# A two-layer decoder with retrieved experts: modulation chunks on GpSimd and ScalarE, 15 weight chunks ahead, and 160 dense tokens in both layers

## The chip, the cores and the metric

The kernel runs on one core of a Trainium2 chip. The metric is the device time of one execution in microseconds. Engines are named as in the profile: PE (matrix multiplications), DVE (VectorE), ACT (ScalarE), POOL (GpSimd) and SP (SyncE, which here only issues transfers). Each engine works through its own instructions in their order and waits for others by semaphores. Transfers between the chip's memory and the core's SBUF are issued by SP, ACT and POOL, and carried by 16 DMA engines.

## The reference

A residual stream of 256 tokens x 1024 channels goes through two layers, in float32. Each layer mixes the tokens, then sends each token through experts that it picks itself (128 x 128 = 16384 experts of one neuron, 8 heads x 16 picks for each token):

```python
def hybrid_layer(x, c_act, ...):
    mod = (c_act @ w_ada + b_ada)[:, None, :]
    sh1, sc1, g1, sh2, sc2, g2 = jnp.split(mod, 6, axis=-1)
    h = rms_norm(x, norm1_g) * (1 + sc1) + sh1
    proj = h @ w_in
    ...
    x = x + g1 * (merged @ w_out)
    h2 = rms_norm(x, norm2_g) * (1 + sc2) + sh2
    x = x + g2 * peer_ffn(h2, peer_wq, peer_sub_keys, peer_down, peer_up)
    return x

def block(t):                      # in peer_ffn
    q = (t @ w_pq).reshape(T, PEER_HEADS, 2, PEER_HALF)
    s = jnp.einsum('thpk,hpnk->thpn', q, sub_keys)
    top_s, top_i = lax.top_k(s, PEER_TOPK)
    cand_s = top_s[:, :, 0, :, None] + top_s[:, :, 1, None, :]
    cand_i = top_i[:, :, 0, :, None] * N_KEYS + top_i[:, :, 1, None, :]
    best_s, best_pos = lax.top_k(cand_s.reshape(...), PEER_TOPK)
    experts = jnp.take_along_axis(cand_i.reshape(...), best_pos, axis=-1)
    gate = jax.nn.softmax(best_s, axis=-1)
    act = jax.nn.gelu(jnp.einsum('td,thkd->thk', t, expert_down[experts]), approximate=False)
    return jnp.einsum('thk,thkd->td', gate * act, expert_up[experts])
```

## The kernel before

**Stages.** Each layer runs through mixing (16 weight chunks of w_in, the attention, convolution and gating work of a plan written out by hand, 8 chunks of w_out), retrieval (16 chunks of w_pq, the scores, the top 16 of each head), and the experts in two loops of 128 weight chunks: down (`chunk_mm`, matmuls in L345) and up (`add` in `combine`, L1137). A chunk is 128 x 1024 float32, 512 KB. Where one stage hands x to the next, ACT and DVE apply the modulation and the norm; below this is called the bridge.

**Dense and gathered tokens.** For T = `DENSE[layer]` tokens the experts' loops multiply with all 16384 experts and weigh the result by the gates (zero where an expert wasn't picked). For the other TS = 256 - T tokens the picked rows alone are gathered: a token has 128 picks, so POOL's indirect transfer (`fetch`, L1038) brings 128 rows, 512 KB, for one token. Rows of down are dotted with the token on DVE (`dot`, L1048), rows of up are weighed and added up on DVE (`add_row`, L1063). Gathered tokens are split into sets of powers of two (88 = 64 + 16 + 8, 96 = 64 + 32); `dot_spread` (L1020) and `spread_picks` (L1025) copy a set's tokens and picks over the partitions by 128/n small POOL transfers each. At chunk 125 of the up loop `folds` (L1143) adds each set's sum into the accumulators, so all rows must be added by then; the last two chunks' matmuls stand behind the folds.

**Buffers for rows.** `free` holds buffers, `fetch` starts a gather for each free one in order of tokens. `begin` is the down chunk at which the picks of the second token block are known; `where` for the first set and the first gathers come 4 chunks later. `start` is the chunk from which the gates of the dense tokens are worked off (`compare`, `factors`, `gate_mm`, `gate_use`). Before it, `dot` is called at the rate `DOT_SLOW` per chunk, after it at `DOT_RATE`.

**Weights.** `Src.seq` is the order of all chunks. They go through a ring of 7 buffers (`RAW`); SP issues the loads, and every second chunk of the experts is issued by ACT. "early" chunks don't use the ring: ten chunks of down (4 to 13 of the loop) are loaded into slots of SBUF (`AHEAD_AT`) while retrieval runs; seven of these slots (`PASSING`) serve as row buffers afterwards. Chunks that are split into a high and a low part (w_in, w_out, w_pq) are cast by ACT (`hi`, L265 and L267) and subtracted by DVE (`lo`, L258 and L260).

**Modulation.** The product c @ w_ada is 48 chunks for each layer, six groups of 8 (SH1, SC1, G1, SH2, SC2, G2). A chunk is multiplied and summed by one DVE instruction (`ada_chunk`, L218). Layer 0's chunks are loaded in its mixing; layer 1's are "asides": 40 in layer 0's experts (21 in the down loop, 19 in the up loop) and 8 in layer 1's, whose loads SP issues between the others.

**Retrieval's picks.** `fills` holds DVE's work for the two token blocks, block 1 first: `cand`, `top_cand`, `ranks`, `match`, `times`, `total` and `gate`; `run_fill` hands out some of it with each down chunk. `gate` (L902 on) subtracts the maximum, lets ACT take the exponential (L905), and sums it on DVE (L906). `expand` (L851) is a POOL cast.

Of the kernel before, what the change touches and what calls it, by code (L numbers as in the profile page):

```python
# [42 lines left out]
DENSE = (168, 160)  # L43
# [34 lines left out]
def hybrid_trunk(ctx: ExitStack, tc: tile.TileContext, x_in, c_in, vec_in, w_ada, w_in, w_out, w_pq,  # L78
# [81 lines left out]
    SLOTS_OPEN = [region(at * S, D) for at in (96, 100, 104)]  # L160
# [22 lines left out]
    class Src:  # L183
# [6 lines left out]
        asides = deque()  # L190
        ring = []
# [24 lines left out]

    def ada_chunk(layer, col, raw):
# [3 lines left out]
        if layer == 0 and col < G1:  # L221
            n = 1
        if (col + 1) % n == 0:
# [7 lines left out]
    def load_more(k):  # L231
        while Src.loaded < len(Src.seq) and (Src.ring[Src.loaded + 1] == Src.ring[Src.loaded]
                                             or Src.ring[Src.loaded] <= Src.ring[k + 1] + RAW - 2):
            dma_ahead(Src.loaded + 1)
# [73 lines left out]
    for layer in range(DEPTH):  # L308
# [3 lines left out]
        if layer == 0:  # L312
# [8 lines left out]
            body += mix(tail[:6], ada(0, [5])) + tail[6:]  # L321
        else:
            body += tail
# [8 lines left out]
        un = mix(un, aside[len(ASIDES_AT[layer]):], 4, 100)  # L332
# [200 lines left out]
    def mixing(layer, qg, update=None, late=None):  # L533
# [260 lines left out]
        other_form(layer)  # L794
        for n in range(2, 16):
            if n >= first:
# [7 lines left out]
        for n, k in enumerate(OUT_ORDER[layer]):  # L804
            if n == 4:
                nc.gpsimd.dma_start(R_KEYS, keys[layer])
            if n < 7:
# [15 lines left out]
    def retrieval(layer, update, late):  # L823
# [29 lines left out]
        narrowed = R_TE[:, 0, 0].rearrange("p j i k -> p (j i k)")[:, :256].rearrange("p (h j i) -> p h j i", h=8, j=2)  # L853
# [47 lines left out]
        def gate():  # L901
# [3 lines left out]
            nc.scalar.activation(sel[:, 2, :], sel[:, 2, :], AF.Exp)  # L905
            nc.vector.tensor_reduce(red[:, :8], g, op=OP.add, axis=AX.X)  # L906
# [46 lines left out]
        for d in range(DC):  # L953
            nc.scalar.activation(R_HX[:, d, :], R_H[:, d, :], AF.Identity, bias=shifts[:, d:d + 1])
        for pair in range(1, 8):
            if pair > 1:
# [7 lines left out]
        def rest():  # L964
            scores(7)
            for b in (1, 0):
# [4 lines left out]
                else:  # L971
                    fill.append((0.3, narrow))
                fill.append((0.95, lambda b=b: cand(b)))
                for h in (0, 4):
                    fill.append((3.8, lambda h=h: top_cand(range(h, h + 4))))
# [414 lines left out]
```

## Time and profile before

| what | us |
|---|---|
| median of 3 runs | 1615.31 (1614.17 to 1615.68) |
| profiled execution | 1619.4 |
| its span | 1617.7 |
| mixing and retrieval of layer 0 | 0 to 188.6 |
| down loop of layer 0 | 188.6 to 523.0 |
| up loop of layer 0 | 523.0 to 849.4 |
| mixing and retrieval of layer 1 | 849.4 to 1002.8 |
| down loop of layer 1 | 1002.8 to 1313.5 |
| up loop of layer 1 | 1313.5 to 1613.6 |

The stages are bounded by the first matmuls of each loop. Such a profile is read from the whole to the part: the busy shares and the transfer rate over the span say which resources are near their limit where; windows laid on the stages say what each carries; the waits of PE say which of them lets it stand still; and the timeline around the end of a stage says what came last.

### The profile page before, as it was taken

Reading aid. Unit: us, or ns where it says so; the run is one execution under the profiler, and the core shown is the slowest. Engines: PE = TensorE matmul, PEld = TensorE weight load, DVE = VectorE, ACT = ScalarE, POOL = GpSimd, SP = SyncE. Lnnn points to the kernel's source line nnn. Section 1 sums busy time; section 2 is a strip of 40 time slices with the busy share of each in tenths; the row PEclk is TensorE's granted clock in tenths of the full one; section 3 lists DMA queues with packets and bytes.
Section 4 is the critical chain, followed back from the end, with each engine's and each line's share of the span. In section 5 each row is a group of like instructions: output and inputs, shape, how many; then the busy total and the mean of one; then the engine's idle time right before and its main releaser. Section 6 shows DMA issues by size and latency. Waiting matters only on the chain.

```text
span 1617.7 us, 29030 instructions
## 1 busy us (share of the span) xinstructions
PE 1550.2 (96%) x11240; PEld 1514.8 (94%) x11240; DVE 1002.7 (62%) x2263; ACT 475.4 (29%) x1356; POOL 518.5 (32%) x467
## 2 busy tenths in 40 slices
PE   7999996999999999998979999989999999999996
PEld 6879996999999999998979899989999999999995
DVE  6778884777777444444436668859777754444435
ACT  2346311466654000000015763115655510000000
POOL 1000125533333544444400001145433444444441
PEclk9999998999999999999979999989999999999997
DMA  9998647999999999999955666499999999999995
GB/s 387 344 361 310 184 151 254 360 419 418 419 418 418 418 419 419 418 419 418 420 216 169 195 231 198 149 387 374 419 418 418 418 419 419 419 419 418 418 419 201
DMA packets 157082, 570.27 MB, mean 353 GB/s; under 512 B 18736, under 2 KB 19312, under 8 KB 155792
## 3 DMA queue, kind: packets, MB, share of 16 engines
q1 hardware_dynamic: 65232, 237.92, 38.4%
q0 software_dynamic: 56144, 201.41, 31.3%
q10 hardware_dynamic: 35568, 129.08, 20.2%
q8 instruction: 88, 1.44, 0.3%
q14 instruction: 50, 0.41, 0.1%
HBM read 562.39 MB, written 3.15 MB: 350 GB/s over the span
## 4 chain that ended last, share of the span: by engine, by line
DMA 41%; PE 35%; issue 11%; POOL 6%; DVE 4%; ACT 2%; POOLq 0%; ACTq 0%; SPq 0%; DVEq 0%
DMA arena<-in_up,arena 28%; PE ch L345 18%; DMA spots<-in_up,arena 6%; POOL arena L1038 5%; DMA arena<-in_down_rows,arena 4%; PE ch L347 2%; PE ch L348 2%; PE ch L349 2%; DMA spots<-in_down_rows,arena 1%; DMA raw<-in_w_ada 1%; PE acc L1143 1%; POOL spots L1038 1%; DVE spots L1063 1%; PE ch L434 1%; PE g L936 1%
## 5 line engine op out<-in xcount | busy, mean ns | idle before, releaser
L345 PE MATMUL ch<-arena,raw 128*128 128x168 f32 (+2 forms) x3936 | 590.1, 309 | 8.2 <-issue 6.3
L1137 PE MATMUL acc<-arena,raw 128*128 128x168 f32 (+1 forms) x4096 | 581.0, 305 | 9.0 <-DMA raw<-in_up 9.0
L1137 PEld LDWEIGHTS acc<-arena,raw 128*128 128x128 f32 x4096 | 578.4, 192 | 11.0 <-DMA raw<-in_up 10.9
L345 PEld LDWEIGHTS ch<-arena,raw 128*128 128x128 f32 x3936 | 563.9, 192 | 15.5 <-issue 9.6
L1063 DVE SCALAR_TENSOR_TENSOR spots<-arena,spots 128x1024 f32<-128x1024 f32 x157 | 201.6, 1284 | 264.0 <-DMA arena<-in_up,arena 263.6
L1038 POOL DMA_INDIRECT arena<-in_up,arena x159 | 220.7, 1388 | 276.6 <-DMA arena<-in_up,arena 222.5
L1038 POOL DMA_INDIRECT arena<-in_down_rows,arena x148 | 163.1, 1102 | 240.1 <-DVE arena L1048 212.5
L1048 DVE SCALAR_TENSOR_TENSOR arena<-arena,spots 128x1024 f32<-128x1024 f32 x148 | 179.8, 1222 | 92.4 <-DMA arena<-in_down_rows,arena 90.7
L1081 ACT ACTIVATE arena<-arena,parts 128x128 f16<-128x128 f16 x164 | 64.6, 394 | 121.5 <-DVE arena L1071 81.2
L1114 ACT ACTIVATE arena<-ch 128x320 f32<-128x320 f32 (+30 forms) x122 | 42.0, 344 | 167.6 <-PE ch L345 141.7
L376 ACT ACT_TABLE_LOAD x6 | 7.7, 1283 | 264.5 <-PE acc L1137 264.4
L347 PE MATMUL ch<-hh,hi 128*128 128x256 f32 x288 | 82.6, 289 | 2.0 <-DVE arena L465 1.9
L348 PE MATMUL ch<-hh,lo 128*128 128x256 f32 x288 | 81.8, 284 | 0.0
L349 PE MATMUL ch<-hh,hi 128*128 128x256 f32 x288 | 81.7, 284 | 0.0
L258 DVE TENSOR_TENSOR lo<-raw,hi 128x1024 fp32r<-128x1024 f32 x42 | 51.2, 1224 | 24.0 <-ACT hi L265 23.8
L1038 POOL DMA_INDIRECT spots<-in_down_rows,arena x36 | 43.9, 1218 | 67.0 <-DVE spots L1048 47.9
L345 PE MATMUL ch<-arena 128*128 128x160 f32 (+2 forms) x384 | 62.7, 323 | 1.7 <-ACT arena L398 1.5
L218 DVE SCALAR_TENSOR_TENSOR raw<-raw,arena 128x1024 f32<-128x1024 f32 x48 | 57.8, 1215 | 9.1 <-DMA raw<-in_w_ada 5.5
L1087 ACT ACTIVATE arena<-arena,parts 128x128 f16<-128x128 f16 x164 | 63.4, 387 | 0.0
L1083 ACT ACTIVATE arena<-arena,parts 128x128 f16<-128x128 f16 x164 | 63.4, 387 | 0.0
L1085 ACT ACTIVATE arena<-arena,parts 128x128 f16<-128x128 f16 x164 | 63.4, 387 | 0.0
L345 PEld LDWEIGHTS ch<-arena 128*128 128x128 f32 x384 | 57.8, 194 | 6.0 <-ACT arena L398 4.0
(227 smaller groups left out, 1716.7 us busy)
## 6 DMA issues: line engine op xcount, KB each, us to landing
raw<-in_up SPq DMA_DIRECT2D x128, 512.0 KB
raw<-in_up ACTq DMA_DIRECT2D x128, 512.0 KB
raw<-in_down SPq DMA_DIRECT2D x118, 512.0 KB
raw<-in_down ACTq DMA_DIRECT2D x118, 512.0 KB
raw<-in_w_ada SPq DMA_DIRECT2D x48, 512.0 KB
aside<-in_w_ada SPq DMA_DIRECT2D x48, 512.0 KB
raw<-in_w_pq SPq DMA_DIRECT2D x32, 512.0 KB
raw<-in_w_in SPq DMA_DIRECT2D x26, 512.0 KB
```

What stands on the lines that cost most here:

```text
L345: nc.tensor.matmul(dst, hi[:, cols], k[0], start=start, stop=stop, **kw)
L347: nc.tensor.matmul(dst, hi[:, cols], k[0], start=start, stop=False, **kw)
L348: nc.tensor.matmul(dst, lo[:, cols], k[0], start=False, stop=False, **kw)
L349: nc.tensor.matmul(dst, hi[:, cols], k[1], start=False, stop=stop, **kw)
L1038: nc.gpsimd.indirect_dma_start(out=held[n], out_offset=None, in_=rows if n >= TS else down_rows[:, :], in_offset=bass.IndirectOffsetOnAxis ...
L1048: nc.vector.scalar_tensor_tensor(row, row, 1.0, R_DX[which(k)[0]], op0=OP.mult, op1=OP.mult, accum_out=R_DOTS[:, k:k + 1])
L1063: nc.vector.scalar_tensor_tensor(R_SUM[s], row, w, R_SUM[s], op0=OP.mult, op1=OP.add)
L1081: nc.scalar.activation(og[0][:, 0, i, :], oh[:, 0, i, :], AF.Copy, scale=parts[:, 0, t + i:t + i + 1])
L1083: nc.scalar.activation(og[1][:, 0, i, :], oh[:, 0, i, :], AF.Copy, scale=parts[:, 1, t + i:t + i + 1])
L1085: nc.scalar.activation(og[0][:, 1, i, :], oh[:, 1, i, :], AF.Copy, scale=parts[:, 0, t + 2 + i:t + 3 + i])
L1087: nc.scalar.activation(og[1][:, 1, i, :], oh[:, 1, i, :], AF.Copy, scale=parts[:, 1, t + 2 + i:t + 3 + i])
L1137: nc.tensor.matmul(acc[d // 2][:, (d % 2) * S:(d % 2) * S + T], u[:, d * P:(d + 1) * P], acts[:, i, :], start=i == 0 and d % 2 == 0, stop= ...
```

## The change

It has five parts, and changes no result.

1. `DENSE` is (160, 160) instead of (168, 160): layer 0 gathers 96 tokens, in sets of 64 and 32.
2. Fifteen early chunks of down instead of ten (chunks 4 to 18). A slot becomes a row buffer as soon as its chunk has been used; all but the first three do. `Src.limits` holds the last early loads back until their slots are free in retrieval. So more buffers are free when the gathers start.
3. Modulation: layer 0 multiplies its own last group (G2) in its experts, beside layer 1's third: 16 asides, 8 in the down and 8 in the up loop. Layer 1's experts have none. The other 40 go through a new function, `pool_ada`: POOL loads a chunk (L229) and multiplies it (L240), ACT sums the product (L241), or one DVE instruction does both (L237). It does layer 1's groups 0 and 1 in layer 0's retrieval, groups 3 and 4 in layer 1's mixing (every second chunk on DVE) and group 5 in layer 1's retrieval, each stream through two buffers; a buffer's next load is issued behind the chunk that used it.
4. `exponents` (the subtraction and the exponential) is a step of its own in `fills` ahead of `ranks`, and `gate` takes its result.
5. Rates: `DOT_SLOW` 0.3 for 0.2, layer 0's `DOT_RATE` 0.9 for 0.8, gates worked off from 6 instead of 4 chunks behind `start`.

```diff
-DENSE = (168, 160)
+DENSE = (160, 160)
...
-DOT_SLOW = 0.2
-DOT_RATE = (0.8, 0.92)
+DOT_SLOW = 0.3
+DOT_RATE = (0.9, 0.92)
...
-AHEAD_AT = (8, 12, 16, 36, 40, 44, 48, 52, 56, 60)
-PASSING = (36, 40, 44, 48, 52, 56, 60)
+AHEAD_AT = (8, 12, 16, 36, 40, 44, 48, 52, 56, 60, 64, 68, 100, 28, 32)
+KEPT = 100
+POOL_AT = ((0, 4), (104, 108))
+FLUSH = 6
-ASIDES_AT = ((16, 18, 19, 20, 22) + tuple(range(46, 127, 5)), (16, 17, 18, 19, 20, 21, 60, 72))
+ASIDES_AT = ((20,) * 6 + (60, 72), ())
+ASIDES_UP = (4, 60)
...
+    def pool_ada(layer, groups, buffers, shared=0):
+
+        jobs = [8 * g + p for g in groups for p in range(8)]
+        bufs = [region(at * S, D) for at in buffers]
+
+        def load(n):
+            if n < len(jobs):
+                nc.gpsimd.dma_start(bufs[n % len(bufs)], w_ada[layer, jobs[n]])
+
+        def step(n):
+            if n == 0:
+                for m in range(len(bufs)):
+                    load(m)
+            raw, col = bufs[n % len(bufs)], jobs[n]
+            if n % 2 < shared:
+                nc.vector.scalar_tensor_tensor(raw, raw, 1.0, cact, op0=OP.mult, op1=OP.mult,
+                                               accum_out=mods[layer][:, col:col + 1])
+            else:
+                nc.gpsimd.tensor_tensor(raw, raw, cact, op=OP.mult)
+                nc.scalar.activation(raw, raw, AF.Copy, accum_out=mods[layer][:, col:col + 1])
+            load(n + len(bufs))
...
-            body += mix(tail[:6], ada(0, [5])) + tail[6:]
-        else:
-            body += tail
+        body += tail
...
-        aside = ada(1, [0, 1, 2, 3, 4] if layer + 1 < DEPTH else [5], "aside")
+        aside = ada(0, [5], "aside") + ada(1, [2], "aside")
...
+        steps, finish = pool_ada(1, [3, 4], POOL_AT[1], 1) if layer else ([], None)
...
-        def gate():
+        def exponents():
             bv = best.rearrange("p (h k) -> p h k", h=8)
             g = sel[:, 2, :].rearrange("p (h k) -> p h k", h=8)
             nc.vector.tensor_sub(g, bv, bv[:, :, 0:1].to_broadcast([P, 8, 16]))
             nc.scalar.activation(sel[:, 2, :], sel[:, 2, :], AF.Exp)
...
+        Src.limits = [Src.starts[layer] + AHEAD_FIRST + n for n in (10, 13)]
+        steps, finish = pool_ada(1, [0, 1] if layer == 0 else [5], POOL_AT[0])
         for pair in range(1, 8):
+            for step in steps[len(steps) * (pair - 1) // 7:len(steps) * pair // 7]:
+                step()
...
+                fill.append((0.3, exponents))
                 fill.append((2.0, ranks))
...
-            elif start is not None and i >= start + 4:
-                want = min(NG, -(-NG * (i - 3 - start) // (G_LAST - 4 - start)))
+            elif start is not None and i >= start + FLUSH:
+                want = min(NG, -(-NG * (i - FLUSH + 1 - start) // (G_LAST - FLUSH - start)))
...
+            n = i - AHEAD_FIRST
+            if 0 <= n < len(AHEAD_AT) and AHEAD_AT[n] >= 28:
+                assert not retired
+                free.append(region(AHEAD_AT[n] * S, D))
+                if AHEAD_AT[n] != KEPT:
+                    passing.append(free[-1])
+                fetch()
```

The order on each engine is set by a scheduler, so some of it can't be read from the diff. POOL at the start of layer 0's gathers, before (`spots<-spots` copies a set's tokens, `pairs<-chosen` its picks; the first row here is the 64-token set):

```order
L1020 DMA spots<-spots 64x1024 x2
L1025 DMA pairs<-chosen 64x2x64 x2
L1038 DMA arena<-in_down_rows,arena 128x1024 x9
L1025 DMA pairs<-chosen 16x2x16 x8
L1020 DMA spots<-spots 16x1024 x8
L1025 DMA pairs<-chosen 8x2x8 x16
L1020 DMA spots<-spots 8x1024 x16
```

The same place after, from the last modulation products on:

```order
L240 TENSOR_TENSOR arena<-arena 128x1024
L892 CAST arena<-arena 128x512 x2
L1074 DMA spots<-spots 64x1024 x2
L1079 DMA pairs<-chosen 64x2x64 x2
L1092 DMA spots<-in_down_rows,arena 128x1024
L1092 DMA arena<-in_down_rows,arena 128x1024 x14
L1079 DMA pairs<-chosen 32x2x32 x4
L1074 DMA spots<-spots 32x1024 x4
```

Fifteen gathers instead of nine stand between the sets, and 4 + 4 small transfers behind them instead of 24 + 24. In layer 1 it was 11 gathers and is 16, with 4 + 4 small ones before and after.

POOL in layer 1's mixing before, from its first tables to the CASTs of retrieval:

```order
L519 AFFINE_SELECT arena<-arena 128x512
L521 MEMSET arena 128x2x2
L806 DMA arena<-in_keys 128x2048
L949 DMA x_dram<-arena 128x2048
L851 CAST arena<-arena 128x512 x8
```

and after, up to the load of the keys (L845):

```order
L240 TENSOR_TENSOR arena<-arena 128x1024
L229 DMA arena<-in_w_ada 128x1024 x2
L240 TENSOR_TENSOR arena<-arena 128x1024
L229 DMA arena<-in_w_ada 128x1024
L240 TENSOR_TENSOR arena<-arena 128x1024
L229 DMA arena<-in_w_ada 128x1024
L240 TENSOR_TENSOR arena<-arena 128x1024
L229 DMA arena<-in_w_ada 128x1024 x2
L240 TENSOR_TENSOR arena<-arena 128x1024
L229 DMA arena<-in_w_ada 128x1024 x2
L240 TENSOR_TENSOR arena<-arena 128x1024 x3
L845 DMA arena<-in_keys 128x2048
```

Of this layer's 16 products 11 stand ahead of the keys, and the other 5 between them and the store of x (L993), that is ahead of the bridge: the second stream, too, was drawn forward out of retrieval.

ACT at the end of layer 1's mixing before (L267 makes the upper halves of w_out's chunks, L265 those of w_pq's, L421 and L440 belong to the bridge):

```order
L741 CAST hh<-arena 128x512
L267 ACTIVATE hi<-raw,vec 128x1024
L265 CAST hi<-raw 128x1024 x2
L421 COPY arena<-mod_108 128x8
L440 ACTIVATE arena<-arena,mod_108 128x256 x2
```

and after (L303, L301, L457 and L476 are the same four):

```order
L241 ACTIVATE arena,mod_107<-arena 128x1024
L303 ACTIVATE hi<-raw,vec 128x1024
L777 CAST hh<-arena 128x512
L241 ACTIVATE arena,mod_107<-arena 128x1024
L303 ACTIVATE hi<-raw,vec 128x1024
L241 ACTIVATE arena,mod_107<-arena 128x1024
L301 CAST hi<-raw 128x1024 x2
L241 ACTIVATE arena,mod_107<-arena 128x1024
L457 COPY arena<-mod_107 128x8
L241 ACTIVATE arena,mod_107<-arena 128x1024
L476 ACTIVATE arena<-arena,mod_107 128x256 x2
```

All 16 sums of this layer stand in ACT ahead of the bridge; the first comes just ahead of the CAST that ran at 870.0 us before, the eighth just behind the work that ran at 903.8.

More of the change, by code (lines that the diff above doesn't have):

```diff
@@ L159, in hybrid_trunk @@
     R_HX = region(88 * S, DC, S)
-    SLOTS_OPEN = [region(at * S, D) for at in (96, 100, 104)]
+    SLOTS_OPEN = [region(at * S, D) for at in (96, 104)]
     SLOTS_UP = [region(at * S, D) for at in (88, 92, 112, 116)]
@@ L190, in hybrid_trunk @@
         asides = deque()
+        limits = []
+        starts = []
         ring = []
@@ L215, in run_fill, with finish @@
             Src.credit -= cost
+    def pool_ada(layer, groups, buffers, shared=0):
[16 more added lines that the diff above has]
+            load(n + len(bufs))
+        def finish():
+            for g in groups:
+                ada_end(layer, 8 * g + 7, 8)
+        return [lambda n=n: step(n) for n in range(len(jobs))], finish
     def ada_chunk(layer, col, raw):
@@ L222, in ada_chunk, with ada_end @@
             n = 1
+        ada_end(layer, col, n)
+    def ada_end(layer, col, n):
         if (col + 1) % n == 0:
@@ L231, in load_more @@
     def load_more(k):
-        while Src.loaded < len(Src.seq) and (Src.ring[Src.loaded + 1] == Src.ring[Src.loaded]
+        while Src.loaded < min([len(Src.seq)] + Src.limits) and (Src.ring[Src.loaded + 1] == Src.ring[Src.loaded]
                                              or Src.ring[Src.loaded] <= Src.ring[k + 1] + RAW - 2):
@@ L806, in mixing @@
                 nc.gpsimd.dma_start(R_KEYS, keys[layer])
+                if finish is not None:
+                    finish()
             if n < 7:
@@ L972, in rest @@
                     fill.append((0.3, narrow))
+                if b == 1:
+                    fill.append((0.0, lambda: Src.limits.clear()))
                 fill.append((0.95, lambda b=b: cand(b)))
@@ L980, in rest @@
                     fill.append((1.6, lambda j=j: total(j)))
-                fill.append((1.0, gate))
+                fill.append((0.7, gate))
                 if b == 1:
@@ L999, in experts @@
         beyond = [region(at * S, D) for at in (80, 84) if at * S >= P * T]
-        passing = [region(at * S, D) for at in PASSING]
-        free = deque([spots[:, n, :] for n in range(len(SETS), 3)] + [region(108 * S, D)] + beyond + passing)
+        passing = []
+        free = deque([spots[:, n, :] for n in range(len(SETS), 3)] + [region(108 * S, D)] + beyond)
         held = {}
@@ L1270, in experts @@
                     due += DOT_SLOW if start is None else DOT_RATE[layer]
-                if start is not None and i < start + 4:
+                if start is not None and i < start + FLUSH:
                     left = [k for k in held if k >= dotted and any(held[k] is r for r in passing)]
-                    due = max(due, min(max(left) + 1, dotted + 3) if left else 0)
-                    assert not left or i < start + 3 or max(left) < due
+                    due = max(due, min(max(left) + 1, dotted + 2) if left else 0)
+                    assert not left or i < start + FLUSH - 1 or max(left) < due
                 while dotted < min(TS, int(due), len(held)):
```

13 lines of the change are left out of this document (11 added, 2 removed).

## The prediction

> **What bounds the kernel now.** I read the page first, then the stages by windows, then the waits of the engine that ends last. The profiled execution took 1619.4 us, of which 1617.7 are the span; the median of the runs is 1615.31, so 4 us come off the sum at the end.
>
> ```profile
> span 1617.7 us, 29030 instructions
> PE 1550.2 (96%) x11240; PEld 1514.8 (94%) x11240; DVE 1002.7 (62%) x2263; ACT 475.4 (29%) x1356; POOL 518.5 (32%) x467
> GB/s 387 344 361 310 184 151 254 360 419 418 419 418 418 418 419 419 418 419 418 420 216 169 195 231 198 149 387 374 419 418 418 418 419 419 419 419 418 418 419 201
> DMA 41%; PE 35%; issue 11%; POOL 6%; DVE 4%; ACT 2%; POOLq 0%; ACTq 0%; SPq 0%; DVEq 0%
> ```
>
> PE is busy 96% of the span, yet the chain that ended last is DMA before PE, and the transfers stand at 418 to 419 GB/s through most of both expert stages. One 512 KB unit (a weight chunk, or the rows of one token) is 0.524 MB, so it costs 1.25 us there. The stages:
>
> ```profile
> 128.00:218.00 90.00, 89.04 (x681) 87.53 (x681) 72.00 (x295) 40.18 (x76) 7.92 (x11) 1.00 0.61 207
> 850.00:940.00 90.00, 89.92 (x698) 83.46 (x697) 59.64 (x118) 56.06 (x119) 0.61 (x1) 1.00 0.57 182
> ...
> 231.40:831.30 599.90, 570.13 (x4123) 565.11 (x4121) 346.18 (x610) 145.57 (x489) 250.56 (x226) 0.98 1.00 399
> 1044.30:1597.20 552.90, 539.42 (x4101) 536.05 (x4099) 324.03 (x558) 133.96 (x465) 242.95 (x200) 0.99 1.02 409
> 231.40:310.00 78.60, 64.45 (x438) 63.04 (x437) 49.36 (x168) 19.81 (x56) 50.77 (x68) 0.91 0.84 288
> 1044.30:1125.00 80.70, 76.56 (x552) 75.20 (x551) 62.09 (x192) 26.53 (x79) 41.08 (x37) 0.94 0.99 368
> ```
>
> After the length stand busy PE, PE loads, DVE, ACT and POOL, the granted clock, the DMA share and GB/s. Retrieval of layer 0 and mixing of layer 1 (the first two rows) have PE full and transfer time to spare. The other rows run from a layer's first gather to the landing of its last row, and over the first 80 us of that. They carry 599.9 x 399 = 239.4 MB in layer 0 and 226.1 MB in layer 1, and layer 0 loses much of its first 80 us (288 GB/s against 368). That the last row ends both layers is seen in the waits and in the timeline of the ends:
>
> ```profile
> PE acc L1143 <- DVE spots L1063: 11.9, 1, 11.9
> PE acc L1137 <- DMA raw<-in_up: 9.0, 6, 3.5
> ...
> PE g L918 <- DVE arena L899: 8.5, 1, 8.5
> PE acc L1143 <- DVE qg L523: 8.5, 1, 8.5
> ```
> ```profile
> 831.78 1.29 DVE L1063 SCALAR_TENSOR_TENSOR spots<-arena,spots 128x1024 f32<-128x1024 f32 x1 [1.06 <-DMA arena<-in_up,arena]
> 833.12 9.55 PE L1143 MATMUL acc<-fold,spots 128*128 128x8 f32 x44 [8.47 <-DVE qg L523]
> 1590.59 9.21 DVE L1063 SCALAR_TENSOR_TENSOR spots<-arena,spots 128x1024 f32<-128x1024 f32 x7
> 1599.86 6.61 PE L1143 MATMUL acc<-fold,spots 128*128 128x32 f32 x30 [11.93 <-DVE spots L1063]
> 1606.28 7.29 PE L1137 MATMUL acc<-arena,raw 128*128 128x160 f32 x32
> ```
>
> The fold in layer 0 is put down to a tiny DVE instruction, but the row's add that began at 831.78 ends at the same moment: both folds wait for the last added row. 11.9 and 8.5 us are only what is left of it at the end; in layer 0 PE also waited 9.0 us for chunks.
>
> **Layer 0's experts.** Dense tokens go from 168 to 160, so gathered tokens from 88 to 96: 8 more rows down and 8 up, +16 units. The modulation chunks there fall from 40 to 16, -24. Five more chunks come early, in retrieval, where the DMA is 39% idle, -5. Together -13 units or -6.8 MB: 232.6 MB are left. At layer 1's mean of 409 GB/s these take 568.7 us, at the plateau's 418 they would take 556. I take 409: after the change layer 0 has layer 1's sets (64 and 32 tokens instead of 64, 16 and 8), and the small transfers that prepare sets fill POOL in the slow stretch:
>
> ```profile
> 260.00:280.00 20.00, 11.18 (x77) 10.61 (x75) 2.83 (x7) 1.73 (x2) 17.05 (x33) 0.84 0.56 145
> ...
> L1025 POOL DMA_DIRECT2D pairs<-chosen x32: 504/548/617, 221.5 to 1061.8; - x32
> L1020 POOL DMA_DIRECT2D spots<-spots x32: 484/518/561, 198.4 to 1071.5; - x32
> ```
>
> Layer 0 issues 26 of each of these 32 and layer 1 only 6; layer 0 will issue 6 too. The 8.5 us wait at L918 lies in this stretch and goes with it; it is not counted beside, because rows, not PE, end the layer. The first gather also comes sooner, since the exponentials now run while DVE ranks, instead of DVE waiting for them:
>
> ```profile
> DVE arena L906 <- ACT arena L905: 17.8, 4, 7.9
> ...
> 231.38 1.04 POOL L1038 DMA_INDIRECT arena<-in_down_rows,arena  x1 [8.64 <-DVE arena L828]
> ```
>
> One of the four waits of each layer's two stands ahead of its first gather. I take the 4.5 us mean, bounds 0 and 7.9. So the rows end at 231.4 - 4.5 + 568.7 = 795.6 instead of 831.3: **-36** (with the plateau's rate -48; with no earlier start and today's 399 GB/s, 583 us, -17). Is PE ready by then? The rows of 160 and 168 tokens:
>
> ```profile
> L1137 PE MATMUL acc<-arena,raw 128*128 128x168 f32 x2048 | 299.4, 310 | 9.0 <-DMA raw<-in_up 9.0
> ...
> L1137 PE MATMUL acc<-arena,raw 128*128 128x160 f32 x2048 | 281.5, 301 | 0.0
> ```
>
> The upper half is 17.9 us shorter on PE, and in layer 1, which has 160 tokens, PE stood 11.9 us before the fold at 1599.86, that is at 1587.9, 543.6 us behind the first gather at 1044.3. From 227 that makes 770, so PE waits for rows and its own saving stays hidden behind them, and the tail behind the fold is as now.
>
> **Layer 1's experts.** No modulation chunks (-8 units) and five more early ones (-5): 219.3 MB, at 409 GB/s 536 us. From 1039.8 the rows end near 1576, ahead of PE's 1587.9, so the 11.9 us go. The 62 matmuls behind that wait took 6.61 + 7.29 = 13.9 us; in the plateau a 20-us window holds 150 of them, so 62 take 8.3, another -5.6. Against it stands the burst: 15 and 16 gathers are sent at one go where 9 and 11 were, and beside the present burst PE stands still for no wait that the trace names:
>
> ```profile
> 1040.00:1060.00 20.00, 15.91 (x104) 14.74 (x102) 15.86 (x109) 1.17 (x3) 12.04 (x13) 0.89 0.93 330
> 1560.00:1580.00 20.00, 20.00 (x150) 20.00 (x149) 7.71 (x6) 0.00 (x0) 8.12 (x6) 1.00 1.03 418
> ```
>
> That is 104 matmuls instead of 150, or 6 us, beside 11 gathers. Five more may cost nothing or 6 us again; by their number it is 3, and I take +4. Sum **-13** (-5 to -18). What is late next is PE itself.
>
> **The modulation chunks on POOL and ACT.** Layer 0's retrieval gets 16 chunks on POOL and ACT, and its mixing loses 8 from DVE. In layer 1, 24 chunks stand between the first w_in chunks and the bridge to retrieval, where none stood: 8 on DVE, 16 on POOL and ACT. Nearest rows:
>
> ```profile
> L851 POOL CAST arena<-arena x16: 611/616/1605, 175.4 to 1009.2; 128x512 f16<-128x512 uint32 x16
> L265 ACT CAST hi<-raw x42: 1029/1047/1052, 128.2 to 992.6; 128x1024 fp32r<-128x1024 f32 x42
> L806 POOL DMA_DIRECT2D arena<-in_keys x2: 562/584/606, 93.0 to 920.1; - x2
> ...
> 870.04 1.05 ACT L265 CAST hi<-raw 128x1024 fp32r<-128x1024 f32 x1 [0.79 <-PE ch L349]
> 903.81 0.58 ACT L551 ACTIVATE arena<-ch 128x512 f32<-128x512 f32 x1
> 944.44 0.20 ACT L421 COPY arena<-mod 128x8 f32<-128x8 f32 x1
> ```
>
> No POOL product of two inputs is in the trace. The CAST makes 512 elements from one input in 0.62 us, so 1024 from two lie between 1.2 (by elements) and 3.2 us (twice the slow CAST); I take 2.4, twice the elements and twice the inputs. A buffer's round is then 2.4 for the product, 1.2 for ACT's sum (the CAST's 1.05 and a read of the accumulator), 0.58 for the next load's issue, and 1.25 to 2.5 for its landing: 6.0 us with the middle. POOL's queue holds each load until ACT has finished, so little of it overlaps. Eight rounds of the first stream, where every second chunk goes to DVE, take 48 us; the order puts the first of their sums just ahead of ACT's CAST at 870.0 and the eighth just behind its work at 903.8. ACT, which sends PE the weights' upper halves, would come out 870 + 48 - 905 = 13 us late. It has 34 of 90 us free in this window and gets some of it back; but the 8 products of the second stream, 4.2 us each (no landing in the way) or 34 us, must also be out by the copy at 944.4. I take **+10**; bounds 0, if the landing is 1.25 and streams interleave, and +27, if products take 3.2 (0.8 x 16 = 13 more) and landings 2.5 (8 x 0.6 = 5). In layer 0, eleven of the 16 products stand between the load of the keys (93.0) and the first CAST (175.4), which feeds DVE: 11 x 4.2 = 46 us in 82, so **0** (-3, if PE gains from the 8 chunks fewer on DVE, to +8).
>
> VectorE and GpSimd meet here. The slow CASTs (1605 ns, not 611) fell beside DVE subtractions with two inputs in SBUF. [...] No run here shows the product yet.
>
> **Sum.** -36 - 13 + 10 + 0 = -39 from 1619.4 is 1580 for a profiled execution, and 1576 by the median of the runs.
>
> **Rivals.**
> (a) *The chunks cost nothing and layer 0 keeps the plateau*: -48 - 15 + 0, 1552. For it: ACT's free 34 us, and POOL's 0.61 us of work in that window. Against: the order in which each load waits.
> (b) *Fewer units, but no better rate.* Layer 0's loss comes from the burst, not from its sets, and 15 gathers prolong it: layer 0 -17, layer 1 -6, mixing +10: 1602. For it: 330 GB/s and PE's 6 us beside layer 1's burst, where the sets are 64 and 32 already. In this case the five early chunks, too, do not do what they are for: while they are used from SBUF, nothing else is to be loaded yet.
> (c) *Slower: POOL's round, in order ahead of ACT's work for PE.* It decides from a product of about 6 us on. At 6.5, layer 1's eight rounds take 8 x 10.1 = 81 us and come out 46 late, I put another 8 on the second stream, and layer 0's eleven, 11 x 8.3 = 91 against 82, add 9: +63 against -49, or 1629. For it: no row has the product, and both engines keep their order. Against: 6.5 us is ten CASTs' time for four times a CAST's work.
>
> **How the numbers follow.** Forecast 0.55, (a) 0.2, (b) 0.15, (c) 0.08, and 0.02 for a result within 0.2% by cancelling; 0.2% is about what a measurement of this kernel can tell from no change. With a share of (b) that goes to nothing (0.02): faster 0.88, same 0.04, slower 0.08. The forecast's own terms give -48 - 18 + 0 - 3 to -17 - 5 + 27 + 8; not all ends come together, so the range goes from (a)'s 1552 less 2 to (b)'s 1602 plus 3: 1550 to 1605.
>
> **What would show it.** Layer 0's window from first gather to last row near 569 us at 409 GB/s (rate kept below 399: (b)); few waits of DVE for pairs at 260 to 285; no PE wait in front of layer 1's fold; a granted clock of 1.0 there; first gathers 4 us sooner after their layer's first dense chunk; PE's waits for the upper halves from ACT in mixing of layer 1, with ACT waiting for POOL's products: none means (a), over 45 us means (c). The forecast is wrong if the product takes under 1.5 or over 4 us, or if PE's stall beside the gathers grows with their number beyond 6 us.

## The result, and the profile after

The changed kernel takes 1637.76 us (median of 4 runs, 1629.99 to 1641.51) against 1615.49 us before: a ratio of 1.013, 95% interval 1.009 to 1.017. It is 22 us slower, where 39 less were forecast, and lies 33 us above the range. The profiled execution took 1636.02 us. Its page:

```profile
span 1634.3 us, 28963 instructions
PE 1526.2 (93%) x11208; PEld 1487.1 (91%) x11208; DVE 1015.3 (62%) x2213; ACT 502.9 (31%) x1400; POOL 624.0 (38%) x515
GB/s 381 352 387 280 211 264 381 321 409 408 409 409 408 408 409 409 409 408 409 400 147 310 231 248 149 147 376 367 409 408 408 409 409 409 408 409 409 408 410 207
DMA 46%; PE 37%; DVE 9%; issue 4%; ACT 2%; POOL 1%; SPq 0%; DVEq 0%; POOLq 0%; ACTq 0%
```

PE has 24 us less work, now that layer 0 has 160 dense tokens as well. But the plateau of transfers, 418 to 419 GB/s before, is at 408 to 409 in both layers, all through both loops. No term of the prediction allowed for that. The windows from a layer's first gather to its last row, and of the first 80 us of that (columns as before):

```profile
231.80:822.00 590.20, 547.83 (x4135) 542.30 (x4134) 336.00 (x590) 138.34 (x470) 244.78 (x202) 0.96 1.01 396
231.80:310.00 78.20, 69.13 (x475) 67.01 (x475) 55.02 (x189) 15.27 (x39) 32.15 (x33) 0.91 0.95 339
...
1052.90:1615.00 562.10, 541.72 (x4103) 537.42 (x4101) 313.45 (x539) 132.97 (x463) 250.05 (x200) 0.98 1.01 399
1052.90:1134.00 81.10, 74.12 (x506) 71.36 (x505) 56.21 (x181) 20.85 (x58) 36.52 (x37) 0.89 0.98 356
```

Layer 0 carries 590.2 x 396 = 233.7 MB, as forecast (232.6), and its first 80 us are better (339 GB/s for 288); it is the rate that keeps its rows late. Layer 1 carries 224.3 MB, not 219.3. PE's waits:

```profile
PE acc L1197 <- DVE qg L559: 28.6, 1, 28.6
PE acc L1197 <- DVE spots L1117: 15.8, 1, 15.8
PE ch L381 <- issue: 15.6, 19, 1.7
PE acc L669 <- ACT arena L659: 9.5, 2, 8.6
```

Both folds (L1197) still wait for rows (the first is put down to a tiny DVE instruction, as before), layer 0's for 28.6 us instead of 8.5; the stall without a named cause has grown from 6.3 to 15.6 us; and PE waits 9.5 us for ACT at L669 in mixing, where before the same matmuls (L633) did not wait for ACT. The times of four marks, read from the traces:

| us | first gather, layer 0 | last up matmul, layer 0 | first gather, layer 1 | last up matmul, layer 1 |
|---|---|---|---|---|
| before | 231.4 | 849.6 | 1044.3 | 1613.6 |
| changed | 231.8 | 837.3 | 1052.9 | 1630.0 |

Layer 0 ends 12.3 us sooner; from there to layer 1's first gather it takes 215.6 us instead of 194.7 (+20.9); and from there to the end 577.1 instead of 569.3 (+7.8). Together +16.4, the difference of the spans.

### The profile page after: what moved, and what is told of

The parts are those of the page before. It is cut to its first block, busy times and chain, and to the rows that moved or that the text cites. A ratio compares the mean times of both kernels' runs of the same rounds, so it can differ in the third digit from the quotient of the medians.

```text
span 1634.3 us, 28963 instructions
## 1 busy us (share of the span) xinstructions
PE 1526.2 (93%) x11208; PEld 1487.1 (91%) x11208; DVE 1015.3 (62%) x2213; ACT 502.9 (31%) x1400; POOL 624.0 (38%) x515
## 3 DMA queue, kind: packets, MB, share of 16 engines
q10 hardware_dynamic: 34704, 125.93, 19.9%
## 4 chain that ended last, share of the span: by engine, by line
DMA 46%; PE 37%; DVE 9%; issue 4%; ACT 2%; POOL 1%; SPq 0%; DVEq 0%; POOLq 0%; ACTq 0%
PE ch L381 27%; DMA arena<-in_up,arena 22%; DMA spots<-in_up,arena 12%; DMA spots<-in_down_rows,arena 6%; DVE spots L1117 2%; DMA arena<-in_w_ada 2%; PE g L1151 1%; DMA arena<-in_down_rows,arena 1%; DMA raw<-in_w_ada 1%; PE ch L470 1%; POOL arena L240 1%; DVE lo L294 1%; DVE raw L251 1%; PE acc L1197 1%; PE acc L1191 1%
## 5 line engine op out<-in xcount | busy, mean ns | idle before, releaser
L381 PE MATMUL ch<-arena,raw 128*128 128x160 f32 (+1 forms) x3776 | 559.6, 307 | 17.2 <-issue 15.6
L1191 PE MATMUL acc<-arena,raw 128*128 128x160 f32 x4096 | 564.2, 301 | 5.9 <-DMA raw<-in_up 5.8
L381 PEld LDWEIGHTS ch<-arena,raw 128*128 128x128 f32 x3776 | 531.7, 192 | 27.2 <-issue 23.6
L1092 POOL DMA_INDIRECT arena<-in_up,arena x160 | 219.3, 1370 | 285.6 <-DMA arena<-in_up,arena 211.1
L1168 ACT ACTIVATE arena<-ch 128x320 f32<-128x320 f32 (+36 forms) x122 | 42.6, 349 | 272.5 <-PE ch L381 217.5
L240 POOL TENSOR_TENSOR arena<-arena 128x1024 f32<-128x1024 f32 x32 | 80.9, 2535 | 50.7 <-DMA arena<-in_w_ada 50.4
L1161 DVE SCALAR_TENSOR_TENSOR arena<-arena,g 128x168 f32<-128x168 f32 (+23 forms) x80 | 39.6, 495 | 77.8 <-ACT arena L1159 74.0
L381 PE MATMUL ch<-arena 128*128 128x160 f32 (+1 forms) x544 | 83.5, 314 | 2.5 <-ACT arena L434 2.4
L1135 ACT ACTIVATE arena<-arena,parts 128x128 f16<-128x128 f16 x160 | 63.7, 398 | 25.7 <-DVE arena L1179 12.9
L1117 DVE SCALAR_TENSOR_TENSOR spots<-spots,arena 128x1024 f32<-128x1024 f32 x30 | 38.5, 1285 | 52.7 <-DMA spots<-in_up,arena 52.6
L229 POOL DMA_DIRECT2D arena<-in_w_ada x40 | 22.4, 562 | 123.0 <-DVE arena L505 33.5
```

The lines of the kernel that those rows point to most:

```text
L240: nc.gpsimd.tensor_tensor(raw, raw, cact, op=OP.mult)
L381: nc.tensor.matmul(dst, hi[:, cols], k[0], start=start, stop=stop, **kw)
L1092: nc.gpsimd.indirect_dma_start(out=held[n], out_offset=None, in_=rows if n >= TS else down_rows[:, :], in_offset=bass.IndirectOffsetOnAxis ...
L1117: nc.vector.scalar_tensor_tensor(R_SUM[s], row, w, R_SUM[s], op0=OP.mult, op1=OP.add)
L1135: nc.scalar.activation(og[0][:, 0, i, :], oh[:, 0, i, :], AF.Copy, scale=parts[:, 0, t + i:t + i + 1])
L1168: nc.scalar.activation(acts[:, i:i + 2, tdone:], v[:, :, tdone:T], AF.Gelu)
```

## The experiments

**Is it the chip?** Both kernels once more, side by side, unchanged:

> The kernel before, once more, on the same chip as the three runs with it. In the profile of the changed kernel the plateau of transfers stands at 408 to 409 GB/s instead of 418 to 419, and a 4096-byte packet takes 159 to 172 ns instead of 159, from the 20th microsecond on, where nothing is changed yet. Theory A (the chip or its state): the plateau here is at 408 too on this chip, and the time is about 1615 + 2.4% of some 1100 us of saturated transfers = 1640. Theory B (the changed kernel brings it about): 418 GB/s and 1615 us here.

> The changed kernel once more, on the same chip. Theory A: the plateau agrees with that of the kernel before on this chip, and the changed kernel is the faster or equal one of the two (at 418 GB/s about 1610). Theory B: 408 GB/s again, 1630 to 1640 us, against 418 for the kernel before.

The kernel before: 1615.55 us (10 runs). The changed one: 1638.27 us (4 runs), 1.0123 of it (1.0095 to 1.0151). The same window of layer 0's up loop, the kernel before first:

```profile
600.00:640.00 40.00, 40.00 (x283) 40.00 (x282) 16.95 (x16) 0.00 (x0) 15.95 (x12) 1.00 1.03 419
```
```profile
600.00:640.00 40.00, 38.76 (x286) 38.51 (x285) 16.42 (x15) 0.00 (x0) 15.82 (x11) 1.00 1.03 409
```

The last two columns are to be read together: the 16 DMA engines are as busy (1.03), and move less. In the trace of the kernel before over 99% of the 4096-byte packets of this window take 159 ns; in the changed one 31% do, and nearly all others 160 to 175. Theory B stands: the kernel brings it about. It shows from 20 to 60 us already (31% of these packets at 159 ns, 96% before), where both kernels issue the same transfers in the same order, so what was left were places. In the compiled programs the table `fold0` grew from 352 to 384 bytes (96 gathered tokens for 88), and everything allocated behind it, the ring of weight chunks first, moved by 32 bytes: from 156928 = 613 x 256 to 156960. The row buffers in `spots` lie behind the ring and always move with it; those in `arena`, the large working area, lie ahead of the table and stayed.

**The place of the ring.** Unused buffers move it, and nothing else; `N` is the number of floats:

```diff
+    pad = consts.tile([P, N], F32, name="pad")
     fold = [consts.tile([P, S - t], F32, name=f"fold{n}") for n, t in enumerate(DENSE)]
```

The first three: the changed kernel with N = 8, the kernel before with N = 8, and the changed kernel with the same pad of 8 ahead of `arena`:

> The changed kernel with one unused buffer of 32 bytes for each partition set aside ahead of the folds' tables. These grew from 352 to 384 bytes with the 96 gathered tokens, and all buffers behind them, the ring of weight chunks first, moved by 32 bytes: from addresses that divide by 64 to ones that do not. The pad moves them to the next multiple of 64. Nothing else differs. Theory (the place of the ring's buffers sets the rate of all transfers): packets of 159 ns throughout, 418 GB/s in the plateau, and 2.4% of some 1100 us of full transfers less: 1608 to 1613 us. Rival (the rate falls for another reason, as the load on POOL's queue): 408 GB/s and 1635 to 1640 us.

> The kernel before with the same pad, which here moves the ring from a multiple of 64 bytes to 32 beside one. Theory: 408 GB/s and some 25 us more, 1635 to 1645 us. Rival: 418 GB/s and 1615 us as ever.

> The changed kernel with the pad ahead of the large working area as well as of the ring, so that both begin at multiples of 64 bytes; the area, into which most gathered rows go, stands 32 beside one in both kernels. If only the ring's place counts: as with the pad behind the area, 1608 to 1613 us. If the rows' place counts too: packets were flat at 159 ns before with the area off by 32, so no further gain is expected from the transfers, and any other difference would be the engines' reading.

The kernel before with the pad takes 1641.92 us, 1.0151 of itself (1.0137 to 1.0165), and its plateau falls to that of the changed kernel: 32 bytes unused cost 25 us against the kernel before on the same chip (1616.49). But a multiple of 64 mends nothing (1636.13 us with the pad behind the area, 1634.36 ahead of it, both at 409 GB/s). So the step is larger. N = 56 and N = 24 behind the area, and N = 24 ahead of it:

> The changed kernel with a pad of 224 bytes, which puts the ring of weight chunks at a multiple of 512. The kernel before has its ring at a multiple of 256 and 418 GB/s; 32 bytes further it had 409 and was 26 us slower; the changed kernel at a multiple of 64 alone still had 409. Theory (the ring must begin at a multiple of 128 or 256 bytes): 418 GB/s, packets of 159 ns, about 1608 to 1613 us. Rival (some other property of the place): 409 GB/s, 1636 us.

> The same with 96 bytes: the ring at a multiple of 128 that is none of 256. If 128 is the step that counts: 418 GB/s; if 256: 409, or something between the two.

> The changed kernel with a pad of 96 bytes ahead of the large working area, which then begins at a multiple of 512, while the ring behind it is at a multiple of 128 that is none of 256. The area receives the gathered rows and the early chunks, somewhat under half of all bytes. Theory (a transfer into a place off 256 bytes costs more on the writing side, and the rate of 418 GB/s is the reading side's, so that it is enough if some half of the bytes go to such places): 418 GB/s. Rival (the ring's place alone counts): 409 GB/s, about 1640 us.

| kernel | ring's address | area's address | GB/s, 600 to 640 us | 4096-byte packets of 159 ns there | time, us | of the kernel before, same chip |
|---|---|---|---|---|---|---|
| before | 613 x 256 | 77 x 256 + 160 | 419 | over 99% | 1615.55 | |
| before, N = 8 | 613 x 256 + 32 | 77 x 256 + 160 | 409 | 31% | 1641.92 | 1.0151 |
| changed | 613 x 256 + 32 | 77 x 256 + 160 | 409 | 31% | 1638.27 | 1.0123 |
| changed, N = 8 | 613 x 256 + 64 | 77 x 256 + 160 | 409 | 28% | 1636.13 | 1.0123 |
| changed, N = 8 ahead of the area | 613 x 256 + 64 | 77 x 256 + 192 | 409 | 32% | 1634.36 | 1.0116 |
| changed, N = 24 | 613 x 256 + 128 | 77 x 256 + 160 | 409 | 34% | 1643.74 (one run) | |
| changed, N = 56 | 614 x 256 | 77 x 256 + 160 | 419 | over 99% | 1619.51 | 0.9998 |
| changed, N = 24 ahead of the area | 613 x 256 + 128 | 78 x 256 | 415 | 75% | 1622.99 (one run) | |

The runs come from several chips, on which the kernel before took 1615.6 to 1620.3 us, so the ratios are surer than the differences of times. In these kernels multiples of 256 bytes decide: with the ring 32, 64 and 128 beside one the rate is 409 GB/s, on one it is 419. With N = 56 the changed kernel is level with the one before (0.9998, 0.9985 to 1.0011). The area, off by 160 in the kernel before, did no harm there; put on a multiple while the ring is off, it brings back 6 of the 10 GB/s (415). The theory on record for that run, by which about half of the bytes may go to places off the step without harm, asked for 418 GB/s, its rival for 409: the result lies nearer to the theory. The step agrees with all eight rows; why a place off it costs anything, and why it costs 2.4% (409 for 419 GB/s), no run shows.

**The bursts.** The gathers paced (four at first, then one more with each chunk of the down loop), alone and with N = 8 and N = 56:

```diff
-                    known_to[0] = SETS[0][1]
+                    known_to[0] = 4
                     fetch()
+                elif begin + WHERE_LAG < i < begin + SETS_KNOWN:
+                    known_to[0] = min(SETS[0][1], known_to[0] + 1)
+                    fetch()
```

> The changed kernel with its first gathers paced: 4 at once, then one more with each chunk of the down loop, instead of 15 or 16 at once. In the changed kernel PE stands still for 12 to 14 us beside each burst. Theory (the number of gathers sent at one go makes the stall): the stall falls under 3 us in each layer. But since the last rows end both layers, and the transfers are full beside the burst, the time moves little: 0 to -6 us. Rival (the stall is from something else that falls there, as the first chunks that come from the ring): the stall stays at 12 us or more.

> Pad and paced gathers together. Pacing alone gave 18 us with the slow transfers (1638 to 1620). If the two are independent: 1608 to 1613 less 15 to 18, 1590 to 1598 us, faster than both kernels. If pacing only gave back what slow transfers lost: 1605 or more.

> Ring at a multiple of 512 and paced gathers. If the two are independent: 1608 to 1613 less the 18 to 19 us that pacing gave twice, 1590 to 1595 us, faster than both kernels. If pacing gains less where transfers are faster: 1600.

1619.98, 1617.19 and **1592.72** us. Pacing takes 18 and 19 us off with slow transfers, not at most 6, and 27 off with fast ones; no kernel that leaves nothing out came out faster than the last one, 0.9831 of the one before (0.9814 to 0.9847). What the burst does, in the changed kernel's profile; first the window around it, then single rows:

```profile
240.00:260.00 20.00, 10.93 (x42) 9.03 (x42) 10.27 (x71) 1.18 (x3) 13.73 (x18) 0.66 1.03 380
...
300.00:320.00 20.00, 20.00 (x162) 19.89 (x161) 19.38 (x38) 9.38 (x32) 11.28 (x8) 1.00 0.91 317
```
```profile
244.44 0.95 POOL L1092 DMA_INDIRECT arena<-in_down_rows,arena  x1 [0.30 <-issue]
245.69 0.95 POOL L1092 DMA_INDIRECT arena<-in_down_rows,arena  x1 [0.30 <-issue]
...
246.10 0.42 PE L381 MATMUL ch<-arena,raw 128*128 128x160 f32 x1 [1.72 <-issue]
246.81 0.23 DVE L873 MATCH_REPLACE8 arena<-arena 128x80 f32<-128x80 f32 x1 [0.64 <-issue]
...
247.54 0.43 PE L381 MATMUL ch<-arena,raw 128*128 128x160 f32 x1 [1.01 <-issue]
```

While POOL sends a gather every 1.25 us, PE gets one matmul out in about that time, and DVE one or two short instructions; 42 matmuls in 20 us, where a window of the plateau holds 150, on a granted clock of 0.66. Why, no record says. The transfers are full meanwhile (380 GB/s), which is why I thought it harmless. But the weight chunks that PE would have freed aren't asked for (in the second trace of this kernel SP issues the first of them at 254.4 us, paced with N = 56 at 240.5), the rows' buffers are all taken, and the transfers fall behind afterwards: 317 GB/s from 300 to 320, for 416 in the paced kernel. With N = 56 the burst costs as much in another form. The waits of that kernel from 232 to 300 us:

```profile
DVE arena L1085 <- DMA pairs<-chosen: 21.2, 1, 21.2
...
PE g L963 <- DVE arena L941: 11.8, 1, 11.8
```

The second set's small transfers stand behind 15 gathers in POOL's queue; DVE waits for them and PE for DVE. Which form comes does not hang on the ring's place. The kernel with N = 24, whose ring is off and whose transfers are slow, has the second form too, and no stall; its window of the burst, and PE's wait behind the bursts of layer 0 and layer 1 (12 us and 18.4):

```profile
240.00:260.00 20.00, 20.00 (x149) 20.00 (x148) 19.62 (x102) 5.03 (x8) 11.98 (x13) 1.00 1.01 391
```
```profile
PE g L963 <- DVE arena L941: 30.4, 2, 18.4
```

All five traces of the changed kernel with a pad of at most 8 and without pacing have the stall (36 to 48 matmuls in the worst 20 us of each layer); the three with 24 or 56 do not. As far as the chips are on record, these three also ran on other ones, so whether the pad or the chip makes the difference is open, and with it why pacing is worth 18 us in one group and 27 in the other. With pacing both forms are gone, and the windows of layer 0 and layer 1 are (N = 56 and pacing):

```profile
231.50:800.00 568.50, 540.93 (x4136) 538.80 (x4134) 335.25 (x590) 136.88 (x469) 247.32 (x202) 0.98 1.02 411
231.50:310.00 78.50, 78.50 (x598) 78.35 (x597) 65.29 (x211) 26.07 (x78) 41.14 (x38) 1.00 1.00 389
1026.80:1571.00 544.20, 534.21 (x4103) 532.55 (x4101) 315.32 (x540) 135.21 (x464) 238.06 (x200) 0.99 1.02 412
```

Layer 0's 568.5 us are the 568.7 of the forecast, though PE waits 26.3 us for them at the fold. From here on this kernel is the base.

**Layer 1's mixing.** First groups 3 and 4 on DVE alone, in the changed kernel and in the base:

```diff
-        steps, finish = pool_ada(1, [3, 4], POOL_AT[1], 1) if layer else ([], None)
+        steps, finish = pool_ada(1, [3, 4], POOL_AT[1], 2) if layer else ([], None)
```

> The changed kernel with all 16 chunks of groups 3 and 4 in layer 1's mixing on DVE (loads still on POOL), so that 8 POOL products and 8 ACT sums go there. Layer 1's mixing was 20 us longer than before (its bridge lags -12 before it and +8 at it). Theory: POOL's rounds, in order ahead of ACT's softmax and its upper halves for PE, cost most of it: 10 to 15 us less time here. Rival: the weight of the work itself (DVE and ACT full) costs it: no gain, or a loss, since DVE gets 8 x 1.2 = 10 us more.

> Besides, the 16 modulation chunks of groups 3 and 4 in layer 1's mixing on DVE. Alone that gave 5 us (1638 to 1633); if layer 1's gathers then come sooner by as much, 1585 to 1590 us. Rival: DVE's own work decides mixing by then, no gain.

1633.23 us against 1638.27, with ratios whose intervals overlap (1.008 to 1.0122 and 1.0095 to 1.0151), and 1593.72 against 1592.72: at best a little, and nothing in the base. So the work was left out, in whole and in part, in layer 1 alone (the sums' places are then set to zero once at the start):

```diff
-            if n % 2 < shared:
+            if groups[0] >= 3:
+                pass
+            elif n % 2 < shared:
```
```diff
                 nc.gpsimd.tensor_tensor(raw, raw, cact, op=OP.mult)
-                nc.scalar.activation(raw, raw, AF.Copy, accum_out=mods[layer][:, col:col + 1])
+                if groups[0] < 3:
+                    nc.scalar.activation(raw, raw, AF.Copy, accum_out=mods[layer][:, col:col + 1])
```

> Ring at a multiple of 512 and paced gathers (1592.7 us), and in layer 1 the products and sums of the modulation groups 3, 4 and 5 left out (the loads stay; the scales and shifts of layer 1's retrieval and its last gate are then wrong). Layer 1's mixing is 17 us longer than before in the kernel with them. Theory (the added work on POOL, ACT and DVE is the cause): those 17 us go, and the first gather of layer 1 comes 15 to 20 us sooner; all of it passes to the end, since rows end the layer: 1573 to 1578. Rival (the 24 added loads, or the transfers' collision with the ring, are the cause): 1590 or more.

> The same, but only the sums on ACT are left out (16 of 1.24 us); POOL's products and DVE's eight chunks stay. If ACT, which waits in its order for POOL and has 20 us more to do ahead of the bridge, is the cause: 10 us or more of the 17 go, 1576 to 1583. [...]

Without products and sums, DVE's eight chunks among them, 1576.33 us, with the loads still there. From layer 0's last up matmul to layer 1's first gather it then takes 194.4 us; the base took 211.9, the kernel before 194.7: the whole 17 us go. Without ACT's sums alone 1595.75 us, and 218.3 in that stretch: nothing goes. ACT's queue, which the prediction priced, is not the cause. Then all 24 chunks on DVE, with no POOL product in layer 1:

```diff
-        steps, finish = pool_ada(1, [0, 1] if layer == 0 else [5], POOL_AT[0])
+        steps, finish = pool_ada(1, [0, 1] if layer == 0 else [5], POOL_AT[0], 2 * layer)
```

(besides the edit for groups 3 and 4 above)

> Ring at a multiple of 512 and paced gathers, and all 24 modulation chunks of layer 1 ahead of its bridge on DVE: no POOL product in layer 1 (loads still on POOL). In the kernel with products DVE's work in layer 1's mixing grew from 68 to 97 us, 10 of them its own 8 chunks and 19 waiting inside instructions: one of 128x4 elements took up to 2.8 us for 0.16, and 5.0 us where the sums were left out. Theory (POOL's products lock DVE out, on the way of the softmax): without them the waiting goes, DVE gets 16 x 1.22 = 20 us of work at places of less haste: 5 to 12 us less than 1592.7. Rival (the amount of DVE's time alone counts): 97 us again, 1592 to 1595.

1595.75 us, and 213.3 in that stretch: the rival holds, the amount of DVE's time counts. From the end of layer 0 to about the bridge's first copy (at 928.2, 908.2, 931.9 and 929.6 us), one row each of the base, without the work, without ACT's sums, and all on DVE (the third number behind the length is DVE's, the fourth ACT's):

```profile
815.00:928.00 113.00, 99.63 (x750) 92.25 (x748) 87.86 (x141) 77.44 (x156) 54.97 (x41) 0.95 0.75 261
```
```profile
813.00:912.00 99.00, 98.90 (x763) 92.14 (x763) 65.60 (x130) 62.61 (x134) 13.76 (x26) 1.00 0.83 303
```
```profile
813.00:929.00 116.00, 98.42 (x714) 89.38 (x713) 93.98 (x138) 60.38 (x123) 52.97 (x41) 0.93 0.75 250
```
```profile
816.00:929.00 113.00, 102.09 (x731) 91.46 (x730) 88.06 (x171) 60.77 (x124) 13.30 (x25) 0.92 0.77 261
```

With the work on POOL, DVE is busy 22 to 28 us longer, though it has only 8 chunks of its own (10 us); with all 24 on DVE it is busy no longer than that. ACT's busy time may be 60 or 77: up to the copy it takes 113 to 119 us with the work, and 95 without. The rest of DVE's time goes into instructions that take longer while POOL multiplies: set against the median of the same form in the run without the work, DVE's instructions in this stretch take 17.2 us longer in the base, 19.9 without ACT's sums, and 1.1 with all 24 chunks on DVE. Two lines of DVE in the changed kernel's trace, and POOL's product (the times are shortest, median and longest in ns):

```profile
L643 DVE TENSOR_SCALAR m<-m x8: 157/164/2878, 70.6 to 899.5; 128x4 f32<-128x4 f32 x8
```
```profile
L294 DVE TENSOR_TENSOR lo<-raw,hi x42: 1205/1225/3433, 129.1 to 1002.9; 128x1024 fp32r<-128x1024 f32 x42
```
```profile
L240 POOL TENSOR_TENSOR arena<-arena x32: 2348/2390/3409, 75.3 to 949.3; 128x1024 f32<-128x1024 f32 x32
```

An instruction of 4 elements for each partition takes 0.16 us, or 2.88 where a product of 2.39 runs from 899.97 to 902.35 us and the instruction ends just behind it. The subtraction with two inputs takes up to 3.43 us instead of 1.2; the six of over 1.4 us all run beside a product, and before the change the longest took 1.37. The trace of before has the same with CASTs on POOL: the slowest, 1605 ns, ran beside that subtraction of 1.37 us. What holds the two engines up, and for which instructions, no run shows further than these times. Beside 16 products DVE's instructions took 17 us longer, nearly as long as it needs to do the products itself (16 x 1.22 = 19.5). No run has POOL's products without DVE's eight chunks, so the cost of each by itself isn't shown.

**Two parts undone in the base.** DENSE (168, 160) as before, without a pad, which puts the ring back to 613 x 256; and the exponentials back next to their sum:

```diff
-DENSE = (160, 160)
+DENSE = (168, 160)
```
```diff
-                fill.append((0.3, exponents))
 ...
-                fill.append((0.7, gate))
+                fill.append((1.0, lambda: (exponents(), gate())))
```

> Paced gathers, and DENSE (168, 160) as before, no pad: the ring then stands at the multiple of 256 where it stood before. 88 gathered tokens in layer 0: 16 units or 20 us of transfers less than with 96, but sets of 64, 16 and 8 with 24 + 24 small transfers, and matmuls of 168. Theory of the prediction (the sets cost layer 0 about 20 us of transfers in its first 80): the two cancel, 1588 to 1600. Rival (the loss came from the burst alone): 20 us of transfers less, 1575 to 1580 if PE's longer matmuls leave it.

> Ring at a multiple of 512 and paced gathers, with the exponentials back behind the ranks and totals, next to their sum. The prediction gave the early exponentials 4.5 us at each first gather. Theory: 5 to 9 us more here. Rival (the first gather stands in its chunk of the down loop and DVE has the time by then: it came at 231.8 us in the changed kernel and at 231.4 before): no difference.

With 168 tokens 1605.79 us (0.994 of the kernel before, for the base's 0.9831): 13 to 18 more. Layer 0's last gather starts at 762.7 instead of 790.4 us and the fold there waits for nothing: rows are ready, and PE sets the end (its matmuls of both loops with weights from the ring take 564.7 us in layer 0, 535.6 in layer 1 with 160 tokens). So neither expectation was quite right: 20 us of transfers do go, but PE takes over. The stretch with the small transfers of the sets is slow with paced gathers too: 203 GB/s from 280 to 300 us, where the base has 419.

With the exponentials back 1601.35 us (0.9897), 9 to 11 more, but not by the mechanism. DVE's waits for them are back (18.7 us in four). But behind its layer's first dense matmul the first gather comes only 2.3 us later in layer 0 (39.1 for 36.8) and 0.3 in layer 1 (41.5 for 41.2). 9.1 us arise between layer 0's last up matmul and layer 1's first dense one, where the scheduler also put instructions of PE, DVE and ACT in another order. Whether the exponentials have a part in that is left open.

## Why the prediction was wrong

62 us lie between forecast and measurement. By the ratios to the kernel before on the same chip, the place of the ring makes 20 us (1.0123 to 0.9998, with the burst) to 30 (1.0015 to 0.9831, paced), the bursts 17 to 27, and together 47 (1.0123 to 0.9831). Some 15 are left in steps of the sum. Against the second trace of the kernel before, from another chip, the base gains 30.5 us by the end of layer 0 (forecast 36), loses 17.2 up to layer 1's first gather (forecast 10) and gains 9.6 behind it (forecast 13).

- *"At layer 1's mean of 409 GB/s these take 568.7 us, at the plateau's 418 they would take 556."* This step failed first, and cost most. Both rates were those of the kernel before, taken as a property of the transfers; the change moved the ring by 32 bytes, and the plateau itself fell to 409. Layer 0's mean came out at 396 GB/s instead of 409, layer 1's at 399. The units were right (233.7 MB for 232.6), and with ring and burst mended so was the time (568.5 us).
- *"Five more may cost nothing or 6 us again; by their number it is 3, and I take +4."* Taken as PE's stall alone, and too small: in the worst 20 us PE got 40 matmuls out in layer 0 and 41 in layer 1, for 109 and 81 before (the window of 104 in the prediction was not the worst). And what follows it, transfers not asked for and the second set's copies late, had no term. Rival (b) named the place; but the kernel with the ring mended and the burst left, which is its case, took 0.9998 of the kernel before, not the 0.992 of its 1602.
- *Layer 1: "No modulation chunks (-8 units)".* Six of the eight were loaded ahead of the first gather already (issued at 995.7 and 1008.6 us in the trace of before), so they were never in the window that was priced: 224.2 MB remain instead of 219.3 (the six are 3.1 MB of that), rows still end last, and PE waits 12.0 us for them in the base, as ever.
- *The chunks on POOL and ACT, +10.* The product was sized right (2.39 us for 2.4), and ACT did wait for POOL (its sums 8.3 us, in seven waits). But layer 1's stretch grew by 17 us in the base and by 21 in the changed kernel (25 in a second trace of it), and by DVE, which the prediction had only in its sentence on the slow CASTs, without a term. That POOL's queue ahead of ACT would decide falls with the run without sums. Layer 0's part, put at 0 (-3 to +8), came near its upper end: its first dense matmul comes 6.4 us later (195.0 us for 188.6). Five of the six subtractions held up beside products lie there, but a run without the products in layer 0 was not made.
- *Exponentials, -4.5 at each first gather.* DVE's waits for them are gone. Layer 0's first gather does come 36.8 us behind the first dense matmul, for 42.8; but that matmul is 6.4 us late, so the gather starts at 231.8 for 231.4. By the run with the exponentials back 2.3 of the 6 us are theirs. In layer 1 the distance is 41.2 us for 41.5, so nothing was gained: the first gather keeps its place in the down loop.
- *PE's saving "stays hidden".* Right in the changed kernel and in the base, where both folds wait for rows. But with paced gathers and a full rate 168 tokens cost 13 us or more: with 8 gathered tokens fewer the rows are early, and PE's longer matmuls end the layer.
- *Rival (c)*, the only one that ended slower, needed a product of 6 us. The result (1638) lies on its side, even beyond its 1629, for other reasons: the product took 2.39 us.

## What to carry over

When a table changes its size, look at where the buffers behind it come to stand: compare packet times of the two traces in a stage that the change doesn't touch before explaining anything else (32 bytes cost 25 us here). Don't send many gathers at one go for the sake of buffers that are free; pace them with the loop that uses up the weights (here 18 to 27 us less). Work moved to POOL beside a busy DVE is not taken from DVE when DVE is held up for as long as it would have worked (here 17 us, for 19.5 of work): count DVE's busy time in the stage, with and without.

## What the runs showed of the hardware

The rate of all transfers hung on where their SBUF buffers begin: 419 GB/s with the ring at a multiple of 256 bytes, 409 at 32, 64 or 128 beside one, and 415 where the working area was on a multiple instead. In five traces PE got out about one matmul, and DVE one or two instructions, for each gather of a burst 1.25 us apart, with no wait in the records; in three others, one of them with its ring at a multiple of 256 and two without, PE held its pace through the same burst (128 to 147 matmuls in the worst 20 us). So the stall does not come from the ring's place; what else separates the two groups, the size of the pad or the chip, wasn't tried. A DVE instruction of 4 elements for each partition took 2.88 us instead of 0.16 beside a POOL product of 2.39.
